# Branch announcements inside the expert passes of a two-layer decoder: all further passes against the first two

## Chip, cores and metric

One core of a Trainium2 chip runs the whole program. The time is the device time of one execution in microseconds; for the kernel before it is the median of three runs. Five engines work side by side: PE (TensorE, matrix products; its weight loads are counted apart as PEld), DVE (VectorE), ACT (ScalarE), POOL (GpSimd, which does almost nothing here) and SP (SyncE, which issues nearly all DMAs). Every engine has its own instruction stream and its own sequencer.

## What is computed

Two decoder layers over 256 tokens of width 1024, fp32. Each layer is a token mixer with four kinds of attention, then cross-attention into 256 memory tokens, then a hierarchical mixture of experts. Only the last part matters here:

```python
g_idx = jnp.argmax(g_logits, axis=-1)                      # 1 of 8 groups per token
top_val, top_idx = lax.top_k(e_logits, TOP_K_IN_GROUP)     # 2 of the group's 4 experts
hid = jax.nn.silu(jnp.einsum('sd,edf->sef', xs, w_gate)) * jnp.einsum('sd,edf->sef', xs, w_up)
return jnp.einsum('sef,efd->sd', hid * gates[:, :, None], w_down)
```

There are 32 experts in 8 groups of 4; each has a gate, an up and a down matrix of 1024 x 256 (1 MB each). How many tokens fall to an expert is known only at run time.

## The kernel before

The two layers run one after the other; each is `attention` and then `moe`. In `moe` the eight groups are served in an order that a table fixes (`SERVED`); `expert(g)` serves one. A pass over a group takes up to 32 tokens for each of its four experts, side by side on the four 32-column quarters of the PE array:

- `up_to` (L1277) multiplies the gathered tokens by the gate and the up weights,
- `silu` on ACT (L1281) and `act` on DVE (L1284) make the hidden values, `turned` (L1290, L427) transposes them,
- `down` multiplies by the down weights (L1306), splits the result in two parts on ACT and DVE (L1310, L1311) and scatters it back to the tokens (L1322, L1327).

The first pass (tokens 0 to 31 of every expert) is always run. If an expert of the group has more than 32 tokens, further passes c = 1 to 7 follow, for tokens 32c to 32c+31. They are nested conditional blocks which `over` writes: the block of pass c is entered if the group's largest count exceeds 32c, and the block of pass c+1 stands inside the block of pass c. So every group carries the code of seven further passes, and a group with no more than 32 tokens for any expert jumps over all of it. PE, ACT, DVE, POOL and SP each take that branch for themselves (line L1368 in the profile, COMPARE_BRANCH).

The count is loaded into a register of each engine (L1397). `foresee` (L1359 to L1365) is the announcement: on PE alone it writes a marker ahead of a later branch, which names that branch and says by the register whether it will be taken. In PE's stream this is two instructions: a register operation (L1363 ALU_OP) and a prefetch hint (L1604 BRANCH_PREFETCH_HINT). The hint tells the sequencer to fetch the code at the branch's target early if the branch will be taken. The announcement needs a label, and the label is handed to the `tc.If` of the block.

The first branch of a group (pass 1) is announced while `up_to` runs, by `tell`. The branch to pass c+1 is announced from inside the block of pass c, by the function that `over` hands to `f`:

- in `whole`, the usual case, `down` calls it between its first and its second half of down products (argument `between`);
- one group of the second layer is in `SPREAD`: group 0, served third. Its passes 1 to 3 are divided. `part` does gate and up and calls the announcement at its very start; `rest` does the down part later, in a second chain of three nested blocks (`top=3`), and announces as `whole` does. Passes 4 to 7 of that group go through `whole`.

Weights come in 1 MB pieces by DMA that SP issues (L275) in the order of one long list, each as soon as a buffer is free. `free` gives the gate and up buffers of a group back after the chain of passes, and the down buffers at the group's end. A pair of comparisons on SP (L274) leaves out experts without tokens.

Of the kernel before, what the change touches and what calls it, by code (L numbers as in the profile page):

```python
# [170 lines left out]
def trunk(ctx, tc, a, out, dbg=None, depth=DEPTH):  # L171
# [922 lines left out]
    def moe(l, pz, pb):  # L1094
# [264 lines left out]
        def foresee(rv, n):  # L1359

            marks[0] += 1
            label = f"m{l}_{marks[0]}"
            tc.mark_branch_hint_location(label, rv > n, engines=[mybir.EngineType.PE])  # L1363
            return label

        def over(rv, f, c=1, label=None, top=7):

            with tc.If(rv > 32 * c, label=label):  # L1368
                nxt = []
                f(c, lambda: nxt.append(foresee(rv, 32 * c + 32)) if c < top else None)  # L1370
                if c < top:
                    over(rv, f, c + 1, *nxt, top=top)

# [30 lines left out]
        def expert(g):  # L1404
# [4 lines left out]
            with tc.manual_schedule(engines={mybir.EngineType.Activation}):  # L1409
# [52 lines left out]
                with apart():  # L1462
                    over(full[g], part if wide else whole, label=label[0])
            free(g, 0, 8)
            pinned[1].close()
            if wide:
                with apart():
                    over(full[g], rest, top=3)
# [28 lines left out]
        for t in range(2):  # L1497
            o, src = ff[:, t], sums(t)
            mv, r = stats(src)
            for h in range(2):  # L1500
                c = slice(h * 512, (h + 1) * 512)
# [106 lines left out]
```

## Time and profile before

| what | value |
|---|---|
| median of three runs | 1011.58 us |
| the three runs | 1015.21, 1004.90, 1011.58 us |
| profiled execution, its own time | 1013.67 us |
| its span, first to last instruction | 1011.9 us |
| lying around the span | 1.8 us |
| PE busy | 923.1 us, 91% of the span |
| bytes moved by DMA | 272.59 MB, 269 GB/s over the span |
| instruction fetches of PE (queue q8) | 86, 1.41 MB |
| PE branches at L1368 that were executed | 30 |
| PE announcements that were executed | 24 |

The expert part of the first layer lies at about 275 to 510 us of the span, that of the second at about 765 to 995 us. A row of the profile names the line, the engine and the operation, what is written and read, and how often; "<-" in a wait names what ended it. A "q" behind an engine's name is its sequencer: PEq L1368 is PE's branch. Queue q1 carries the program's data, queue q8 the code that PE fetches, queue q14 the code of other engines. A hint's line in the profile is L1604, since it is placed when the program is closed.

### The profile page before, as it was taken

How to read it: one execution, taken by the hardware profiler on the slowest of the kernel's cores; microseconds unless marked ns; L12 is line 12 of the kernel's file. 1: busy time of each engine (PE TensorE's matmuls, PEld its weight loads, DVE VectorE, ACT ScalarE, POOL GpSimd, SP SyncE). 2: the span in 40 equal slices, each digit the busy share in tenths (PEclk: the TensorE clock that was granted, in tenths of full speed). 3: DMA queues.
4: the chain of work that ended last, by engine and by line, in shares of the span. 5: the costliest groups of instructions: out<-in, count | busy, mean ns of one | idle time of the engine just before them, and what ended most of it. 6: DMA issues, size and time to landing. Idle time of an engine off the chain costs nothing. (4 is left out here: it accounts for less than half of the span.)

```text
span 1011.9 us, 19936 instructions
## 1 busy us (share of the span) xinstructions
PE 923.1 (91%) x7948; PEld 688.2 (68%) x7948; DVE 503.3 (50%) x1258; ACT 340.9 (34%) x736; POOL 0.2 (0%) x4
## 2 busy tenths in 40 slices
PE   7899999999998688989899999999999888997885
PEld 7888987898754354856368899789885564444541
DVE  5755755544653333323466575554465414644434
ACT  5454855343411121011144475435442121121111
POOL 0000000000000000000000000000000000000000
PEclk9999999999999899999999999999999999999998
DMA  9842334538769988999786244553784994719995
GB/s 351 343 147 99 134 128 161 209 125 331 293 268 422 424 348 367 424 425 420 250 336 229 108 147 180 174 208 110 288 351 196 421 387 183 318 58 421 422 363 203
DMA packets 43774, 272.59 MB, mean 269 GB/s; under 512 B 4832, under 2 KB 5344, under 8 KB 13280
## 3 DMA queue, kind: packets, MB, share of 16 engines
q1 hardware_dynamic: 43472, 270.26, 68.2%
q8 instruction: 86, 1.41, 0.5%
q14 instruction: 72, 0.59, 0.2%
q10 hardware_dynamic: 144, 0.33, 0.1%
HBM read 269.52 MB, written 1.05 MB: 267 GB/s over the span
## 5 line engine op out<-in xcount | busy, mean ns | idle before, releaser
L432 DVE SCALAR_TENSOR_TENSOR wl<-main,wh 128x1024 fp32r<-128x1024 f32 (+1 forms) x93 | 112.2, 1211 | 112.1 <-ACT wh L431 111.9
L431 ACT ACTIVATE wh<-main 128x1024 fp32r<-128x1024 f32 (+1 forms) x93 | 97.3, 1052 | 116.5 <-PE bank L438 68.3
L437 PE MATMUL bank<-xh,wh 128*128 128x256 f32 x368 | 108.8, 298 | 5.6 <-ACT xh L488 3.6
L438 PE MATMUL bank<-xl,wh 128*128 128x256 f32 x368 | 105.8, 288 | 1.0 <-DVE xl L432 0.6
L439 PE MATMUL bank<-xh,wl 128*128 128x256 f32 x368 | 104.9, 286 | 0.0
L1277 PE MATMUL bank<-ext,xg 128*32 128x256 f32 x912 | 88.2, 392 | 2.9 <-DMA ext<-exp 2.8
L1327 DVE TENSOR_TENSOR ff<-ff,bank 128x512 f32<-128x512 f32 x84 | 53.2, 681 | 49.9 <-PE bank L1322 49.9
L437 PEld LDWEIGHTS bank<-xh,wh 128*128 128x128 f32 x368 | 71.1, 194 | 7.0 <-ACT xh L488 4.1
L438 PEld LDWEIGHTS bank<-xl,wh 128*128 128x128 f32 x368 | 71.3, 194 | 2.2 <-DVE xl L432 0.9
L439 PEld LDWEIGHTS bank<-xh,wl 128*128 128x128 f32 x368 | 71.4, 194 | 0.1
L1277 PE MATMUL bank<-main,xg 128*32 128x256 f32 x640 | 66.1, 384 | 2.4 <-DMA main<-exp 2.4
L460 ACT ACTIVATE xg<-bank,prmb 128x128 f32<-128x128 f32 x64 | 24.0, 456 | 123.3 <-PE bank L1227 117.2
L1310 ACT ACTIVATE y<-bank,sm 128x512 fp32r<-128x512 f32 (+1 forms) x46 | 30.7, 669 | 103.5 <-PE bank L1306 76.1
L1322 PE MATMUL bank<-y,dt 128*128 128x512 f32 (+1 forms) x184 | 56.9, 422 | 7.9 <-DVE y L1311 7.2
L1306 PE MATMUL bank<-ext,dn 128*32 128x512 f32 (+1 forms) x212 | 46.6, 670 | 17.5 <-PEq L1368 6.8
L437 PE MATMUL bank<-wh,oh 128*128 128x512 f32 (+1 forms) x160 | 60.9, 380 | 0.0
L439 PE MATMUL bank<-wh,ol 128*128 128x512 f32 (+1 forms) x160 | 59.1, 369 | 0.0
L1322 PEld LDWEIGHTS bank<-y,dt 128*128 128x128 f32 x184 | 29.6, 188 | 43.2 <-ACT y L1310 16.4
L438 PE MATMUL bank<-wl,oh 128*128 128x512 f32 (+1 forms) x160 | 59.0, 369 | 0.0
L1277 PEld LDWEIGHTS bank<-ext,xg 128*32 128x32 f32 x912 | 42.6, 112 | 22.5 <-issue 4.7
L1227 PEld LDWEIGHTS bank<-dn,xhat 128*128 128x128 f32 x448 | 51.1, 192 | 5.8 <-issue 4.9
L1227 PE MATMUL bank<-dn,xhat 128*128 128x128 f32 x448 | 53.7, 278 | 0.0
(300 smaller groups left out, 2008.7 us busy)
## 6 DMA issues: line engine op xcount, KB each, us to landing
ext<-exp SPq DMA_DIRECT2D x75, 1024.0 KB, 16.6
main<-exp SPq DMA_DIRECT2D x54, 1024.0 KB, 12.8
main<-wsq SPq DMA_DIRECT2D x33, 1024.0 KB, 5.0
main<-win SPq DMA_DIRECT2D x22, 1024.0 KB, 6.8
M<-exp SPq DMA_DIRECT2D x17, 1024.0 KB, 15.0
VM<-exp SPq DMA_DIRECT2D x8, 1024.0 KB, 17.1
xx<-exp SPq DMA_DIRECT2D x7, 1024.0 KB, 14.0
M<-wsq SPq DMA_DIRECT2D x5, 1024.0 KB, 7.1
```

Of the source, the lines that this page charges most:

```text
L431: ACT.activation(hi, src, AF.Copy, scale=scale)
L432: DVE.scalar_tensor_tensor(lo, src, scale, hi.bitcast(F32), op0=ALU.mult, op1=ALU.subtract)
L437: PE.matmul(psum, lh, rh, start=first, stop=False, skip_group_check=True)
L438: PE.matmul(psum, lh, rl, start=False, stop=False, skip_group_check=True)
L439: PE.matmul(psum, ll, rh, start=False, stop=last, skip_group_check=True)
L460: ACT.activation(dst, src, AF.Identity, bias=b, scale=g)
L1227: PE.matmul(b[:, k * 128:(k + 1) * 128], xhat[:, t, c:c + 128], d[:, t], start=(t == 0 and k == 0), stop=(t == 1), skip_group_check=True)
L1277: PE.matmul(pg[m * i:m * i + m, which * S:(which + 1) * S], x[:, k, m * i:m * i + m], w[:, k], start=(k == 0), stop=(k == 7), skip_group_c ...
L1306: PE.matmul(b[m * i:m * i + m], ht[:, f * 128 + m * i:f * 128 + m * i + m], w[:, o:o + n], start=(f == 0), stop=(f == 1), skip_group_check ...
L1310: ACT.activation(hi, b, AF.Copy, scale=gate)
L1322: PE.matmul(bs[t], dt[:, t * 128:(t + 1) * 128], y[i], start=(i == 0 and not held), stop=(i == 1), skip_group_check=bool(held))
L1327: DVE.tensor_add(o, o, bs[t])
```

## The change

`over` hands out the announcement only in the block of pass 1. The branch into pass 1 (announced by `tell`) and the branch into pass 2 (announced from the block of pass 1) stay as they were. The branches into passes 3 to 7 are no longer announced, and their blocks get no label.

```diff
             with tc.If(rv > 32 * c, label=label):
                 nxt = []
-                f(c, lambda: nxt.append(foresee(rv, 32 * c + 32)) if c < top else None)
+                f(c, lambda: nxt.append(foresee(rv, 32 * c + 32)) if c == 1 else None)
                 if c < top:
                     over(rv, f, c + 1, *nxt, top=top)
```

On PE 81 pairs of instructions leave the program, 162 in all: five for each of the sixteen groups (blocks of passes 2 to 6) and one in the second chain of the divided group. No other engine gains or loses an instruction. Everything that stands behind a removed pair moves up in PE's stream: ten instructions for each group, 152 by the last one.

The first place is the divided group of the second layer on PE: the end of pass 2's gate and up part, the branch into pass 3, that pass's start. (f is the choice of tokens that gathers them from xhat; xx holds the gathered tokens.) Before:

```order
L1277 MATMUL bank_3_64<-M_0_119,xx_0_69 32x256
L1277 MATMUL bank_3_64<-R_0_76,xx_0_69 32x256
L1368 COMPARE_AND_BRANCH
L1363 REGISTER_ALU
L1604 BRANCH_PREFETCH_HINT
L1227 MATMUL bank_5_66<-f_61_0_13925,xhat_0_77 128x128 x8
L1227 MATMUL bank_2_63<-f_61_0_13925,xhat_0_77 128x128 x8
```

And now:

```order
L1277 MATMUL bank_3_64<-M_0_119,xx_0_69 32x256
L1277 MATMUL bank_3_64<-R_0_76,xx_0_69 32x256
L1368 COMPARE_AND_BRANCH
L1227 MATMUL bank_5_66<-f_61_0_13805,xhat_0_77 128x128 x8
L1227 MATMUL bank_2_63<-f_61_0_13805,xhat_0_77 128x128 x8
```

The pair behind the branch is gone; it announced the next branch, the one into pass 4. The same pair is gone one block earlier, where it announced the branch into pass 3. Nothing else changes its place relative to its neighbours.

The second place is the divided group's later chain on PE, pass 2's down part, between its two halves (VM and ext hold down weights). Before:

```order
L1306 MATMUL bank_2_63<-ext_1_13934,f_61_1_13926 32x512
L1363 REGISTER_ALU
L1604 BRANCH_PREFETCH_HINT
L1306 MATMUL bank_7_68<-VM_0_75,f_61_1_13926 32x512
L1306 MATMUL bank_7_68<-KT_0_74,f_61_1_13926 32x512
```

And now:

```order
L1306 MATMUL bank_2_63<-ext_1_13814,f_61_1_13806 32x512
L1306 MATMUL bank_7_68<-VM_0_75,f_61_1_13806 32x512
L1306 MATMUL bank_7_68<-KT_0_74,f_61_1_13806 32x512
```

The pair between the halves is gone; it announced the chain's branch into pass 3.

## The prediction

> **What bounds the kernel now.** I read the page first, then the chain of work that ended last, then busy time and DMA by stretch for the second layer's experts, then PE's branches one by one.
>
> ```profile
> span 1011.9 us, 19936 instructions
> ...
> 910.52 0.75 PE bank L1322 x2
> ...
> 912.46 20.29 DMA main<-exp
> ...
> 985.96 6.99 DMA VM<-exp
> ...
> 992.99 1.90 PE bank L1306 x10
> ```
>
> The chain says that the end is set by weights that stream in from 912 to 993 us, and that the stream started when PE's work of 910.5 us had given buffers back. So the question for the second layer is what delays PE before 911 us.
>
> ```profile
> 840.00:846.00 6.00, 5.50 (x104) 3.09 (x100) 0.00 (x0) 1.75 (x5) 0.00 (x0) 1.00 0.01 4
> ...
> 890.00:900.00 10.00, 8.41 (x140) 4.43 (x142) 1.45 (x6) 2.27 (x6) 0.00 (x0) 1.00 0.01 2
> ...
> 912.00:930.00 18.00, 13.85 (x171) 8.67 (x163) 6.94 (x22) 2.16 (x6) 0.00 (x0) 0.94 1.01 421
> ```
>
> The last column is GB/s. DMA moves 421 GB/s from 912 on, but 4 GB/s at 840 to 846 and 2 at 890 to 900: all buffers are full, and DMA waits for PE. PE's own waits from 770 to 907 us are twelve rows, none for a DMA; the first and the last of them:
>
> ```profile
> PE bank L1306 <- ACTq L1368: 3.4, 2, 1.7
> ...
> PE bank L1322 <- ACT y L1310: 0.3, 1, 0.3
> ```
>
> In that stretch a microsecond that PE loses is a microsecond lost at the end; after 912 us DMA is the limit and short PE waits are covered.
>
> **The change, part by part.** First, what runs of it. Executed branches and announcements on PE, whole program, then the divided group's stretch from 807 to 868 us:
>
> ```profile
> L1368 PEldq COMPARE_BRANCH  x30: 68/365/5925, 282.9 to 989.4; - x30
> ...
> L1604 PEldq BRANCH_PREFETCH_HINT  x24: 32/38/44, 278.9 to 982.5; - x24
> ...
> L1368 PEldq COMPARE_BRANCH  x8: 68/78/367, 807.9 to 861.4; - x8
> ...
> L1604 PEldq BRANCH_PREFETCH_HINT  x5: 32/32/35, 808.2 to 856.3; - x5
> L1363 PEldq ALU_OP  x5: 37/37/37, 808.1 to 856.2; - x5
> ```
>
> Sixteen of the 24 are the groups' first announcements, which stay. Five lie in the divided group: three in its first chain (ahead of passes 2, 3 and 4) and two in its second. The remaining three belong to the three groups that run one further pass; each is announced from the block of pass 1 and stays. So the change takes away three executed announcements: two in the first chain (ahead of passes 3 and 4), one in the second (pass 3). Two of the three branches are not taken: the count is above 96, the code goes straight on, and such branches lasted 68 to 78 ns. They lose nothing. **One taken branch loses its announcement**: the one into pass 4, at 846.1 us, which jumps over the code of four passes.
>
> *The announcements themselves.* 3 x (0.037 + 0.032) = 0.2 us of PE's sequencer. In the first chain it runs ahead of products still queued; I count -0.1 us.
>
> *The branch at 846.1 us.* Its row, and what PE's code queue q8 did between the announcement and the branch:
>
> ```profile
> L1368 PEldq COMPARE_BRANCH  x1: 367/367/367, 846.1 to 846.1; - x1
> ...
> DMA packets 12, 0.04 MB, mean 3 GB/s; under 512 B 8, under 2 KB 8, under 8 KB 8
> ...
> q8 instruction: 1, 0.02, 0.5%
> ```
>
> One code fetch in 12.8 us, and the branch then took 0.37 us. No taken long jump without an announcement exists in this trace. The nearest rows are announced ones whose fetch came only after the branch had begun: one with DMA idle (377.5 us, 11 GB/s), two with DMA full (446.1 us at 425 GB/s, 921.4 us at 419).
>
> ```profile
> L1368 PEldq COMPARE_BRANCH  x1: 3631/3631/3631, 377.5 to 377.5; - x1
> ...
> DMA packets 5, 0.04 MB, mean 11 GB/s; under 512 B 1, under 2 KB 1, under 8 KB 1
> ...
> q8 instruction: 1, 0.02, 1.7%
> ...
> L1368 PEldq COMPARE_BRANCH  x1: 5811/5811/5811, 446.1 to 446.1; - x1
> ...
> DMA packets 343, 2.51 MB, mean 425 GB/s; under 512 B 38, under 2 KB 38, under 8 KB 38
> ...
> L1368 PEldq COMPARE_BRANCH  x1: 5925/5925/5925, 921.4 to 921.4; - x1
> ...
> DMA packets 344, 2.52 MB, mean 419 GB/s; under 512 B 38, under 2 KB 38, under 8 KB 38
> ```
>
> Bounds: 0.37 us if the target is there anyhow, 5.93 us at worst. I take 3.63 us, since DMA is idle around 846 us too (3 and 11 GB/s). Not all of it is lost. PE went on after the branch only when DVE had made the last hidden values:
>
> ```profile
> L1368 PEldq EVENT_SEMAPHORE  x1: 51/51/51, 847.6 to 847.6; - x1
> ...
> PE bank L1290 <- DVEq L1368: 0.9, 1, 0.9
> ```
>
> The branch would end at 846.07 + 3.63 = 849.7 us instead of 846.4; PE's next step stood at 847.6. So the loss is 849.7 - 847.6 = **2.1 us**; by the bounds 0 to 846.07 + 5.93 - 847.6 = 4.4 us. It lies in the stretch where PE sets the pace, and the buffers that the group gives back at 848 us come that much later, so I let it through whole.
>
> [...]
>
> *Everything behind moves up.* PE's code comes in pieces. In the second layer's attention part, a stretch with no branches:
>
> ```profile
> 526.50:753.40 226.90, 223.83 (x1509) 196.92 (x1508) 131.95 (x300) 113.47 (x255) 0.00 (x0) 0.99 0.56 203
> ...
> q8 instruction: 12, 0.20, 0.3%
> ```
>
> 1509 products and 1508 weight loads in 12 fetches are one fetch for 251 instructions. Each group stands 10 instructions earlier than the one before it, 152 at the end, so where an announcement and its branch fall in such a piece is dealt anew: whether the next sequential piece is fetched ahead of the announced one or not. PE's waits at these branches now, of the whole program, then the longest branch that ended in a wait for ACT, and two single waits for PE's own branch:
>
> ```profile
> PE bank L1306 <- PEq L1368: 12.1, 6, 4.0
> PE bank L1306 <- ACTq L1368: 11.7, 7, 1.7
> ...
> L1368 PEldq COMPARE_BRANCH  x1: 2416/2416/2416, 786.7 to 786.7; - x1
> ...
> PE bank L1306 <- ACTq L1368: 1.6, 1, 1.6
> ...
> PE bank L1306 <- PEq L1368: 3.5, 1, 3.5
> ...
> PE bank L1306 <- PEq L1368: 2.3, 1, 2.3
> ```
>
> Seven groups wait some 1.7 us (11.7 in 7), ended by ACT's own turn at the block's end, though PE's branch took up to 2.4 us; the dearest wait for PE's own branch, behind the 5.81 us one, is 4.0 us; those at 377.5 and 398.3 us are 3.5 and 2.3. So a re-dealt group costs between 1.7 and 4.0 us, up to 2.3 either way. I expect the 5.81 us branch to gain that (-2.3), one or two others to lose as much, and DMA to hide part of both in the first layer. I take 0, with -4.6 and +4.6 as the ends: two groups either way (2 x 2.3).
>
> *Sum.* -0.1 + 2.1 + 0 = +2.0 us. On the profiled execution, 1013.67 us (1011.9 of span and 1.8 around it), that is 1015.7. That execution lies 2.1 us above the median of the runs shown; on the median, 1011.58, the sum gives **1013.6 us**. The three runs before differ by 10.3 us, about 1%, which is what a measurement of this kernel can tell from no change.
>
> **Rivals.**
>
> [...]
>
> *The new layout gives back more than the branch takes.* The three dear waits for PE's own branch fall to the 1.7 us of the others: (4.0 - 1.7) + (3.5 - 1.7) + (2.3 - 1.7) = 4.7 us, time 1013.6 - 4.7 = 1008.9. For it: they are the three dearest, and a re-dealt fetch is likelier to come out nearer the common case. Against: all three lie in the first layer, where DMA is full for most of the time and PE waits for weights besides.
>
> *The layout turns against it: slower by over 1%.* When the sequential piece is asked for just ahead of the announced one, and DMA is full, the announced piece comes second and the branch takes 5.8 us or more. Price 2.3 us for each group that waits 1.7 now. It decides from four of the seven: 2.0 + 4 x 2.3 = 11.2 us, time 1022.8. For it: two branches show it already (446.1 and 921.4 us, 5.8 and 5.9 us). Against: the groups after 912 us are covered by DMA, which leaves five that could pay.
>
> **How the numbers follow.** The forecast, no change that can be told, centred at +2.0 us: 0.62. Target in the store: 0.13. Layout gives back: 0.15. Layout turns against: 0.10. The first two and four fifths of the third lie within 1% (0.62 + 0.13 + 0.12 = 0.87), less 0.02 on each side for the spread of the runs: 0.83. Faster by over 1%: 0.03 + 0.02 = 0.05. Slower by over 1%: 0.10 + 0.02 = 0.12. Range: down to 1013.6 - 4.6 (layout) less half of the runs' spread (5.1), 1004; up to 1013.6 + 2.3 (the dearer branch) + 4.6 (layout), 1020.5, the spread left out there since both are worst cases.
>
> **What would show it.** In the changed profile: 21 announcements at L1604 instead of 24, 30 branches still. The branch after pass 3 of the divided group, near 846 us, should last 3.6 us instead of 0.37, with one q8 packet inside it, and the wait of L1290 behind it should be a wait for PE's own sequencer. The stream of weights that starts at 912 should start some 2 us later and run the same 81 us. [...] If the times of other groups' first branches have moved by more than that in sum, the layout and not the lost announcement tells the result.

## The result, and the profile after

| | before | changed |
|---|---|---|
| median of ten runs each | 1011.56 us | 1021.18 us |
| lowest and highest | 1004.90 and 1015.40 us | 1015.79 and 1025.11 us |
| ratio to before, 95% interval | | 1.0103, 1.0078 to 1.0129 |
| profiled execution, its own time and span | 1013.67 and 1011.9 us | 1022.55 and 1020.8 us |

The change makes the kernel 9.6 us slower at the medians. The forecast was +2.0 us, and its range ended at 1020.5 us. Here and below, a ratio with its interval is worked out over all fast executions and is not the quotient of the two medians beside it; one execution of the first experiment, 1539 us long at a granted clock of 0.555, is left out.

First the rows on PE's sequencer that answer to those of before: the announcements, all branches, and then four single branches. The columns are the count and the shortest, median and longest duration in ns.

```profile
L1604 PEldq BRANCH_PREFETCH_HINT  x21: 28/39/44, 279.4 to 991.7; - x21
...
L1368 PEldq COMPARE_BRANCH  x30: 65/574/6570, 283.5 to 996.9; - x30
...
L1368 PEldq COMPARE_BRANCH  x1: 3711/3711/3711, 378.1 to 378.1; - x1
...
L1368 PEldq COMPARE_BRANCH  x1: 1730/1730/1730, 452.0 to 452.0; - x1
...
L1368 PEldq COMPARE_BRANCH  x1: 3350/3350/3350, 848.3 to 848.3; - x1
...
L1368 PEldq COMPARE_BRANCH  x1: 3408/3408/3408, 911.6 to 911.6; - x1
```

There are 21 announcements and 30 branches, as forecast. The branch that lost its announcement (848.3 us) took 3.35 us instead of 0.37. Several branches that were announced before and after differ all the same; two of them show both directions: the one at 446.1 us fell from 5.81 to 1.73 us, and the one at 904.7 us rose from 0.47 to 3.41 us.

Next, PE's waits of the changed kernel around the lost announcement, and its stretches there (in a stretch's row, the third number from the end is the granted clock, the last one GB/s):

```profile
PE bank L1290 <- DVE dt L1266: 2.6, 1, 2.6
...
845.00:852.20 7.20, 4.28 (x76) 2.11 (x68) 0.80 (x3) 0.38 (x1) 0.00 (x0) 1.00 0.02 6
852.20:859.00 6.80, 6.10 (x30) 1.67 (x34) 1.85 (x7) 1.07 (x2) 0.00 (x0) 0.50 0.94 346
859.00:866.00 7.00, 6.42 (x46) 2.49 (x42) 4.52 (x12) 1.63 (x3) 0.00 (x0) 1.00 1.00 420
```

PE was idle for 2.6 us where it had been idle for 0.9. For the 6.8 us that follow, the granted clock is 0.50. Before, the same work had the full clock; the row of before, and then the down products of that place in the changed kernel and in before:

```profile
848.40:855.20 6.80, 6.22 (x43) 2.52 (x43) 3.60 (x11) 1.76 (x3) 0.00 (x0) 1.00 0.96 367
```

```profile
L1306 PE MATMUL bank<-ext,f x16: 593/1061/1062, 853.6 to 859.3; 128*32 128x512 f32 x16
```

```profile
L1306 PE MATMUL bank<-ext,f x16: 592/592/617, 849.3 to 852.4; 128*32 128x512 f32 x16
```

30 products against 43 in 6.8 us, and one product in 1.06 us against 0.59. From the second chain's first branch to its second, PE took 9.43 us (852.14 to 861.57) where it had taken 6.62 (848.00 to 854.62): 2.8 us more, in a place where not one instruction was added.

The lag of the changed trace behind the trace of before, measured at the same branch in both, adds up so:

| branch, time before | lag | what grew it |
|---|---|---|
| 282.9 us, first of the first layer | 0.55 us | start of the run |
| 398.3 us, first layer's fifth group | 1.81 us | |
| 446.1 us, the sixth | 5.98 us | +4.2: behind the branch that is now 6.57 us and was 4.13 |
| 469.0 us, the seventh | 3.06 us | -2.9: the branch that is now 1.73 us and was 5.81 |
| 767.9 us, first of the second layer | 1.72 us | |
| 846.1 us, the lost announcement | 2.25 us | |
| 848.0 us, the next | 4.14 us | +1.9: the branch |
| 854.6 us, the one after | 6.95 us | +2.8: products at half clock |
| 904.7 us, fourth served group | 6.95 us | |
| 921.4 us, fifth served group | 9.12 us | +2.2: the branch that is now 3.41 us |

The weight stream that waits for PE moved with it. Before, it was already at 352 GB/s from 907 us on, earlier than the 912 us that the prediction read off the chain; in the changed trace it is idle until 912 and full from 918:

```profile
907.00:910.00 3.00, 3.00 (x29) 0.93 (x18) 2.59 (x14) 0.91 (x2) 0.00 (x0) 1.00 0.99 352
```

```profile
907.00:912.00 5.00, 4.95 (x36) 1.92 (x28) 1.92 (x3) 1.38 (x2) 0.00 (x0) 1.00 0.00 0
912.00:918.00 6.00, 2.76 (x26) 0.97 (x28) 4.36 (x16) 0.36 (x1) 0.00 (x0) 1.00 0.32 89
918.00:920.00 2.00, 2.00 (x16) 0.83 (x8) 1.56 (x5) 0.91 (x2) 0.00 (x0) 1.00 1.06 442
```

So the two traces tell of 1.9 + 2.8 + 2.2 us in the second layer. What they can't tell by themselves is whether the first layer's rows are typical, since each is one execution.

### The profile page after: what moved, and what is told of

Same layout as the page of the kernel before. It is cut to its first block, busy times and chain, and to the rows that moved or that the text cites. A ratio compares the mean times of both kernels' runs of the same rounds, so it can differ in the third digit from the quotient of the medians.

```text
span 1020.8 us, 19930 instructions
## 1 busy us (share of the span) xinstructions
PE 924.9 (91%) x7948; PEld 686.3 (67%) x7948; DVE 503.7 (49%) x1258; ACT 341.0 (33%) x736; POOL 0.2 (0%) x4
## 3 DMA queue, kind: packets, MB, share of 16 engines
HBM read 269.52 MB, written 1.05 MB: 265 GB/s over the span
## 5 line engine op out<-in xcount | busy, mean ns | idle before, releaser
L1306 PE MATMUL bank<-ext,dn 128*32 128x512 f32 (+1 forms) x212 | 46.3, 640 | 14.8 <-PEq L1368 8.1
L1311 DVE SCALAR_TENSOR_TENSOR y<-bank,sm,y 128x512 fp32r<-128x512 f32 (+1 forms) x46 | 33.3, 725 | 47.7 <-ACT y L1310 44.5
```

The source lines that it names most:

```text
L1306: PE.matmul(b[m * i:m * i + m], ht[:, f * 128 + m * i:f * 128 + m * i + m], w[:, o:o + n], start=(f == 0), stop=(f == 1), skip_group_check ...
L1311: DVE.scalar_tensor_tensor(lo, b, gate, hi.bitcast(F32), op0=ALU.mult, op1=ALU.subtract)
```

## The experiments

Each kernel has its own runs of the kernel before on the same chip; ratios are to those. "Stands elsewhere" means the place of an announcement in PE's instruction stream. I moved it by code that never runs, such as blocks of pass 7, so that what PE executes stays the same. Where a kernel has lines added, the rows' line numbers are higher by as many (L1308 and L1307 are L1306, L1291 is L1290).

### One part alone, and the change with one part undone

The first kernel is that of before with all 24 announcements in their place, but those ahead of passes 3 to 7 always say that the code goes straight on:

```diff
-                f(c, lambda: nxt.append(foresee(rv, 32 * c + 32)) if c < top else None)
+                f(c, lambda: nxt.append(foresee(rv, 32 * c + 32 if c == 1 else 0)) if c < top else None)
```

> The kernel before, with every instruction in its place; the announcements inside the blocks of passes 2 to 6 now always say that the branch will not be taken. So the code's layout is that of before and only the taken branch of the divided group (near 846 us) loses its early fetch. Theory A (the lost announcement counts, and PE's products run slowly for a while after the idle time): that branch takes 3.4 to 3.7 us, the products behind it (L1306) take 1.06 us each for some 5 us, and the kernel is 4 to 5 us slower than before, about 1016. Theory B (the layout makes the loss, the branch costs its wait alone, 2 us as predicted): 1013.5. Theory C (all of the loss is layout, the announcement did nothing): 1011.5, branch 0.4 us.

Measured: 1012.94 us against 1010.23, ratio 1.0037 (1.0018 to 1.0055), 2.7 us at the medians. The branch took 3.36 us at 837.5 us, PE idled 2.6 us behind it, and of the 6.8 us that followed half ran at half clock (mean 0.75):

```profile
L1368 PEldq COMPARE_BRANCH  x1: 3357/3357/3357, 837.5 to 837.5; - x1
...
PE bank L1290 <- DVE dt L1266: 2.6, 1, 2.6
...
841.50:848.30 6.80, 6.22 (x36) 1.97 (x37) 1.73 (x7) 1.42 (x3) 0.00 (x0) 0.75 0.94 358
```

So the lost announcement by itself costs about a third of the change's 1.03%. The rest must have another cause, and the new places of the code are the nearest.

The second is the changed kernel with that announcement kept (in the divided group's first chain, ahead of pass 4):

```diff
+        def tell_of(c, top):
+            return c == 1 and top == 7 or c == 3 and wide_now[0]
-                f(c, lambda: nxt.append(foresee(rv, 32 * c + 32)) if c == 1 else None)
+                f(c, lambda: nxt.append(foresee(rv, 32 * c + 32)) if tell_of(c, top) else None)
```

> The changed kernel with one announcement back, the one into pass 4 of the divided group; one announcement of that group's second chain, whose branch is not taken, is left out, so that all code behind stands where the changed kernel has it. Theory A: the branch near 848 us takes 0.4 us again, PE's products behind it stay at 0.6 us, and 4 to 5 us of the changed kernel's loss come back: about 1016.5. Theory B: only 2 us come back: about 1019. Theory C: nothing, 1021. All: the branch of the next group (near 905 to 912 us) still takes 3.4 us, since its announcement and its branch stand where the changed kernel has them.

Measured: 1015.22 us against 1010.23, ratio 1.0076 (1.0048 to 1.0104). The branch took 1.59 us and not 0.4: its code packet came 11.7 us after the announcement, where it came after 7.8 us before. PE idled 0.9 us, with no half clock behind it. The branch at 903.9 us still took 3.43 us. What is left, 0.76%, does not come from this announcement: from its branch to the second chain's second one 8.6 us passed, as in before. What came back, 0.27%, is less clear: with six executions the interval overlaps that of the changed kernel.

The third gives the divided group of the changed kernel four announcements back that decide nothing (eight instructions, two of them executed), so that the branch at 911.6 us stands eight places later:

```diff
+            return c == 1 or top == 3 and c == 2 or 3 < c < top and wide_now[0]
```

> The changed kernel with eight instructions more in the divided group: three pairs in blocks that never run, one pair in the second chain (its branch is not taken). Passes 3 and 4 stay unannounced. Everything from the group served fourth on stands eight instructions later. That group's taken branch, 3.4 us in the changed kernel against 0.47 before, stands at the edge of a code piece there by my count. If the place in the piece makes that branch slow, it takes 0.5 us here and the kernel gains 2.5 to 3 us on the changed one, about 1018.5; if the loss follows from something earlier (a later DMA, the branch at 848), it stays at 3.4 us and 1021.

Measured: 1018.6 us against 1010.23, ratio 1.0102 (1.0072 to 1.0131). The branch fell to 0.47 us, so its place alone had lost its announcement. Whether that place is the edge of a code piece is not shown: the expectation has it from a count of mine, and no trace tells where a piece ends. In the changed kernel no code packet came between announcement and branch; here one did:

```profile
DMA packets 0, 0.00 MB, mean 0 GB/s; under 512 B 0, under 2 KB 0, under 8 KB 0
```

```profile
L1372 PEldq COMPARE_BRANCH  x1: 466/466/466, 908.1 to 908.1; - x1
...
q8 instruction: 1, 0.02, 1.1%
```

The time did not fall, though. The branch at 968.1 us now took 5.9 us (0.71 in the changed kernel). The eight places need not be the reason: in the changed kernel with two announcements moved, below, where it stands 512 places later and not eight (near two code packets, by the estimate given there), it took 6.0 us. The price of the one branch isn't told by this run.

### Which branch the layout costs

The branch into pass 2 of the first layer's fourth group (377.5 us before) took 3.6 us in before's profile and 3.7 in the changed one, so the two traces show no difference there. In the profile of the first experiment, whose layout is that of before, it took 0.43. The two profiles from the announcement to the branch, before and then that one:

```profile
q1 hardware_dynamic: 152, 1.02, 47.6%
q14 instruction: 1, 0.01, 0.7%
```

```profile
q1 hardware_dynamic: 146, 0.99, 46.1%
q8 instruction: 1, 0.02, 1.2%
q14 instruction: 1, 0.01, 0.6%
```

With the one the announced code came in time (the q8 row), with the other no packet came before the branch. Two kernels move this announcement and bring the code behind back to its place. (The first also moves the two groups ahead up, by 10 and 20 places, as the change does; their branches took 1.08 and 2.55 us, against 1.04 to 1.56 and 2.01 to 2.45 in the seven profiles of before's layout. The second also moves the next group, by 10.) The edit to before that both share, with the first one's numbers (`SPARE`: unread transposes in a group's pass 7; `BARE`: groups whose announcements ahead of passes 3 to 7 are left out; none of either runs there):

```diff
+BARE = [(0, 0), (0, 1), (0, 2)]
+SPARE = {(0, 3): 15}
...
+                f(c, lambda: nxt.append(foresee(rv, 32 * c + 32)) if c < top and (c == 1 or not bare[0]) else None)
...
+                elif top == 7 and spare[0]:
+                    b = banks.get()
+                    for _ in range(spare[0]):
+                        PE.transpose(b[:, 0:128], ident, ident)
+                    banks.put(b)
```

> The kernel before, with every announcement that it executes. Only code that never runs is shorter in the first three groups of the first layer (30 instructions) and as much longer in the fourth, so that the fourth group's announcement into its second further pass stands 30 instructions earlier, where the changed kernel has it; all groups behind stand where they stand before. Theory (the place of the announcement costs, not its absence): that branch, 0.43 us in two profiles of this layout and 3.63 in one, takes 3.6 to 3.8 us and PE idles 3.5 us there; the time is 1.5 to 4 us above before, since some runs of before lose it too. Rival (the rest of the change's cost lies behind this group): the branch may take what it likes, the time is that of before within 1 us.

Measured: 1012.75 us against 1009.30, ratio 1.0038 (1.0019 to 1.0058), 3.5 us. The row of the branch and PE's wait behind it:

```profile
L1370 PEldq COMPARE_BRANCH  x1: 3411/3411/3411, 374.7 to 374.7; - x1
...
PE bank L1308 <- PEq L1370: 3.3, 1, 3.3
```

Nothing that PE executes differs from before; 30 instructions of place cost as much as the lost announcement of the first experiment. The other way:

```diff
+BARE = [(0, 3), (0, 4)]
+SPARE = {(0, 2): 10}
```

> The other way: the same announcement 20 instructions later than before (the next group's 10 later), by code that never runs; all behind stands where it stands before. Theory: the branch takes 0.43 us in this layout in every run, PE's idle time there falls under 0.5 us, and the time is 0.5 to 3 us below before. Rival: the time is that of before within 0.5 us.

Measured: 1009.20 us, ratio 1.0000 (0.9979 to 1.0020); the branch took 0.43 us. The expected gain of 0.5 to 3 us isn't there. The reason stands in the other profiles of before's layout: of seven, the fetch was missed in one, which was the profile that I predicted from. Measured in the trace, from the start of the last code packet to this announcement, in all fourteen profiles of the study:

| from the last code packet to the announcement | profiles | branch |
|---|---|---|
| 0.82 to 0.98 us (four kernels with the changed kernel's place) | 4 | 3.41 to 3.81 us |
| 1.46 us (before) | 1 | 3.63 us |
| 1.60 to 1.92 us | 9 | 0.43 to 0.56 us |

An announcement that came less than 1.5 us after the start of the last code packet was lost at this branch. The changed kernel's place lies ahead of that edge, before's place lies close to it. Why it is lost isn't shown: the packets took 0.94 to 0.96 us, so in before's profile the last one had been over for 0.5 us. Nor is the edge the same elsewhere. At the branch of 846.1 us an announcement 1.46 us behind a code packet was kept (0.37 us, in the first run with eight steps of DVE, below); at that of 921.4 us announcements 1.05 to 2.58 us behind one were lost in the changed kernel and the three made from it (3.2 to 3.8 us).

The changed kernel with both of its misplaced announcements moved (the first layer's fourth group's and the second layer's fourth served group's), all else left alone or moved by 256 or 512 places (near one and two code packets, by an estimate from the 251 products and weight loads for one fetch in the trace of before):

```diff
+SPARE = {(0, 2): 25, (0, 3): 103, (1, 2): 4, (1, 3): 124}
```

> The changed kernel, without the three announcements, with code that never runs added at four places, so that two announcements stand elsewhere: the first layer's fourth group's 50 instructions later, the second layer's fourth served group's 8 later; all other groups stand in their pieces as in the changed kernel. Theory: the two branches fall from 3.7 and 3.4 us to under 0.5, only the lost announcement is left, and the time is 3 to 5 us above before (ratio 1.003 to 1.005, as where that announcement alone was made idle) and not 9.6. Rival (other branches, or the new order of fetches at large, cost): the time stays at that of the changed kernel, 1.009 to 1.011.

Measured: 1014.75 us against 1009.30, ratio 1.0049 (1.0030 to 1.0067): half of the change's cost is gone, without one announcement given back. The two branches took 0.43 and 0.46 us. The one that has no announcement took 3.90, PE idled 3.2 us, and 3.4 us at half clock followed (granted clock 0.50 from 848.5 to 851.9 us). What is left agrees with the first experiment (1.0037), within both intervals.

```profile
L1369 PEldq COMPARE_BRANCH  x1: 432/432/432, 377.4 to 377.4; - x1
...
L1369 PEldq COMPARE_BRANCH  x1: 459/459/459, 905.7 to 905.7; - x1
...
L1369 PEldq COMPARE_BRANCH  x1: 3901/3901/3901, 843.2 to 843.2; - x1
```

And a version that uses this: all announcements that are executed, and the dear ones moved. (The edit moves the groups behind the first layer's sixth by 272 places, 16 more than the 256 of the kernel above, so they don't stand as the expectation says.)

```diff
+BARE = [(0, 3)]
+SPARE = {(0, 2): 10, (0, 4): 96, (0, 5): 35, (1, 3): 99, (1, 4): 29}
```

> The kernel before with all its announcements, and code that never runs added at five places, so that the dear branches' announcements stand elsewhere: the first layer's fourth group's 20 instructions later, its sixth group's 186 later in its piece (just ahead of the piece's end, as in the three groups with the cheapest branches), the second layer's fifth served group's 198 later; all others stand in their pieces as before. Theory: the three branches fall to 0.43, 1.7 and under 3.5 us (0.43 or 3.6, 5.8 and 5.9 before), and the time is 3 to 6 us below before. Rival (weights set the pace in the first layer and behind 912 us of the second, so that PE's waits there are covered): within 1 us of before.

Measured: 1007.81 us, ratio 0.9983 (0.9967 to 1.0000). The three branches took 0.56, 1.46 and 1.01 us, about as expected or shorter, but the gain is 1.5 us at the medians and not 3 to 6, at the edge of what the runs can tell. So most of PE's waits there seem to be covered by the weight stream, as the rival had it. At the first layer's sixth group the traces show it: from that branch to the next group's it took 24.2 us here and 23.7 in the first experiment, where the branch took 5.84 us and not 1.46.

### What a short stall costs PE

The half clock behind the stall was seen in the trace; these kernels test that it is the idle time that brings it, and its price. They are the kernel before, with steps of DVE ahead of the second chain's first transposes, and no change to the branches:

```diff
                 def rest(c, hint):
+                    if c == 1:
+                        for _ in range(8):
+                            DVE.tensor_scalar(hw[c], hw[c], 1.0, None, op0=ALU.mult)
```

> The kernel before with eight extra DVE steps (times 1.0) on the hidden values of pass 1 of the divided group, just ahead of the second chain: PE has to wait some 2 us longer at L1290 near 848 us, with no branch and no code fetch involved. PE's code is unchanged. Theory A: the wait of 0.9 us becomes 2.5 to 3.3 us, the products behind it run at 1.06 us instead of 0.6 for some microseconds, and the kernel loses 4 to 5 us. Theory B: it loses what the wait grows by, 2 us, and the products stay at 0.6 us.

Measured: 1017.28 us, ratio 1.0079 (1.0055 to 1.0102). PE's idle time grew by 3.7 us (0.87 to 4.54), but the stretch to the next branch by 6.5 (13.1 for 6.62). Then once more, with two kernels beside it on the same chip: two steps instead of eight, and eight steps with twelve unread transposes on PE meanwhile.

> The eight steps alone once more, on the same chip as the two others: 5 to 8 us over before (1.005 to 1.008), 3.7 us of it delay, the rest products at half rate.

> The kernel before, with two idle steps of DVE instead of eight at the same place. Theory: PE's idle time of 0.87 us grows to some 1.8 us, its products behind stay at full rate, and the time rises by the 0.9 us of the two steps (ratio 1.000 to 1.002). Rival (any stall there costs near twice its length): 1.8 us.

> The kernel before, with eight idle steps of DVE (a product by 1.0) ahead of the divided group's last hidden values, as in the run that lengthened PE's idle time there to 4.5 us and took 6.5 us more for the stretch up to the next of its passes; now PE does twelve transposes that nobody reads in that time. The code behind is brought back to its place by code that never runs. Theory (PE's products run at half rate after the idle time): the same delay of 3.7 us, PE idle at most 1.5 us at a time, no product at half rate behind it, and 3.5 to 4.5 us in all over before, 2 to 3 us less than the eight steps without the transposes. Rival (the delay itself costs all of it): as with the eight steps alone.

Measured: eight steps 1016.85 us against 1009.86, ratio 1.0073 (1.0058 to 1.0088); two steps 1.0003 (0.9985 to 1.0021); with twelve transposes 1.0067 (1.0045 to 1.0088). The wait ahead of the transposes and the stretch behind it, for eight steps, two steps, and twelve transposes:

```profile
PE bank L1290 <- DVE prmb L1462: 4.5, 1, 4.5
...
844.70:851.50 6.80, 6.02 (x30) 1.68 (x34) 0.86 (x2) 1.07 (x2) 0.00 (x0) 0.50 1.02 428
```

```profile
PE bank L1290 <- DVE prmb L1462: 1.9, 1, 1.9
...
845.90:852.70 6.80, 6.14 (x42) 2.54 (x43) 3.16 (x10) 1.76 (x3) 0.00 (x0) 1.00 0.98 410
```

```profile
PE bank L1291 <- DVE prmb L1470: 2.2, 1, 2.2
...
847.00:850.40 3.40, 3.25 (x16) 0.79 (x20) 0.00 (x0) 0.10 (x1) 0.00 (x0) 0.50 1.00 424
```

1.9 us of idle time left the clock alone. The twelve transposes ran one behind another in 1.5 us, less than I had counted on, and left 2.2 us: 3.4 us at half clock instead of 6.8, and a time that can't be told from that of eight steps. By the time alone the rival stood; the clock's row says that the test was too weak. So the same with 28 transposes:

```diff
+                        b = banks.get()
+                        for _ in range(28):
+                            PE.transpose(b[:, 0:128], ident, ident)
+                        banks.put(b)
```

> As the run with eight idle steps of DVE and twelve transposes, but with 28 transposes on PE: twelve took 1.5 us and left PE idle for 2.2 us, behind which its products ran at half rate for 3.4 us all the same. By 0.125 us each 28 last 3.5 us and leave under 0.5 us. Theory (half rate after idle time): no product of the divided group at half rate, and the stretch from the first branch of its second chain to the next takes 10.3 us (6.62 before, and 3.7 of delay) instead of 11.9 with twelve and 13.2 with none; the time is 3.5 to 4.5 us above before (ratio 1.003 to 1.005). Rival (the delay alone costs it): the ratio stays at 1.007.

```profile
PE bank L1291 <- DVE prmb L1470: 0.4, 1, 0.4
...
848.70:855.50 6.80, 6.17 (x42) 2.55 (x43) 2.07 (x4) 1.76 (x3) 0.00 (x0) 1.00 1.01 426
...
L1307 PE MATMUL bank<-ext,f x16: 592/592/617, 849.7 to 852.7; 128*32 128x512 f32 x16
```

Measured: 1013.52 us against 1009.73, ratio 1.0041 (1.0017 to 1.0065). The stretch took 10.30 us, as expected: 6.62 and 3.7 of delay. The rival's ratio of 1.007 lies just outside the interval. The same eight steps of DVE cost 0.73 to 0.79% with PE idle and 0.41% with PE busy. The difference is 3 to 4 us; the products at half clock make 2.9 us of it in the traces (a stretch of 13.2 us against 10.3).

## Why the prediction was wrong, step by step

**What bounds the kernel** was right. A microsecond that PE lost between 768 and 912 us came out at the end: in the last experiments 3.7 us of delay cost 3.8 us at the medians (28 transposes), and a stretch 6.6 us longer cost 7.0 (eight steps). The two traces alone would not show it: the lag of PE's branches is 9.1 us at 921 us, falls to 5.2 at 946, and is 8.9 us at the end of the span.

**What runs of the change** was right: three executed announcements fewer, two of them idle (their branches last 65 ns each), one that matters.

**The branch at 846.1 us** was right in its own duration (3.63 us forecast, 3.35 measured) and in the shift that follows (2.1 forecast, 1.9 measured). Its path was longer than forecast: L1290 was to wait for PE's own sequencer, but it waited for DVE's step L1266, which had itself waited for PE's branch:

```profile
851.82 0.29 DVE L1266 TENSOR_SCALAR dt<-cst 128x256 fp32r<-128x256 f32 x1 [1.48 <-PEq L1368]
```

The rival in which the branch stays near 0.4 us without its announcement (in the chances "target in the store", 0.13) fell: it took 3.35 us here and 3.36 in the first experiment. No run shows a store of PE's code or what it holds; what the traces show is code packets, one between announcement and branch before (841.1 us; branch 0.37 us) and one inside the branch in the changed trace (849.4 us).

**The first step that failed** is "Not all of it is lost ... So the loss is 849.7 - 847.6 = 2.1 us": the stall was priced at its own length. PE's idle time of 2.6 us was followed by 6.8 us at half clock, 2.8 us more. In the profiles of the first experiment and of the changed kernel with two announcements moved it is 3.4 us instead of 6.8. Alone, the announcement cost 0.37%, 2.7 us at the medians. The trace of before had this price in it, behind the very row that gave the 3.63 us: after a wait of 3.5 us the products took 1.06 us each, and 0.59 only some 4 us later.

```profile
381.71 0.92 PE L1306 MATMUL bank<-main,dn 128*32 128x512 f32 x1 [3.48 <-PEq L1368]
382.43 1.06 PE L1306 MATMUL bank<-main,dn 128*32 128x512 f32 x1
385.55 0.59 PE L1306 MATMUL bank<-main,dn 128*32 128x512 f32 x1
```

**The second step that failed** is "I take 0, with -4.6 and +4.6 as the ends: two groups either way". The dear branch at 446.1 us did gain (5.81 to 1.73 us), as expected, and others lost. But I took the 3.63 us of the branch at 377.5 us for a price that before always pays, and even listed it among the waits that a new layout could give back. It was an accident of the one profiled execution: six of seven profiles of that layout show 0.43. The change moves this announcement 30 instructions up, to where it was lost in all four profiles with that place, and that move cost 0.38%.

If the two prices add, 0.37% and 0.38% make 0.75 of the 1.03%; with both misplaced announcements moved the changed kernel comes to 1.0049, near the 1.0037 that is left for the lost announcement. The price in time of the second layer's fourth served group's branch was not separated; in the traces its stretch to the next group took 18.9 us in the changed kernel and 20.6 in the second experiment, against 16.7 to 17.1 in the twelve profiles where that branch was short. The branches at 398.3 and 446.1 us nearly cancel: with the changed kernel's layout the stretch behind the first took 51.6 to 51.9 us in four profiles of four, against 47.6 to 48.6 in the other ten, and the stretch behind the second 20.0 to 20.1 us against 22.9 to 24.2. The branch at 966.5 us (2.95 to 0.71) was not separated either.

The rival "the layout turns against it" was nearest, 1022.8 us with a chance of 0.10, but its mechanism was another. It had four groups paying 2.3 us each because the announced piece came second, its reading of the branches at 446.1 and 921.4 us, each with one code packet between announcement and branch and a second inside the branch (443.7 and 449.5, 919.0 and 925.0 us); here two announcements were lost altogether, and only the branch at 398.3 us looks like that rival (2.4 us longer).

How long PE can idle before its products slow down is open. The half clock came in stretches of 3.4 us (before, 381.8 to 385.2 us: granted clock 0.51) and 6.8 us (changed, 852.2 to 859.0 us: 0.50). Idle times of 2.2 and 2.6 us were enough for it, in the kernel with twelve transposes and in the changed one, while 3.2 us ahead of 915.6 us in the changed trace brought none (its row from 912 to 918 us has clock 1.00). The same place in the second experiment's profile, idle for 3.3 us, did bring one (clock 0.51 from 908.0 to 911.5 us). What decides between them isn't shown.

## What to carry to other kernels

Price a stall of PE with what follows it: here idle times from 2.2 us on were followed by a half clock in most cases (eight of the ten in the traces of before and of the changed kernel), and two of its stretches of 6.8 us cost 2.8 and 2.9 us. Add that, or give PE something to do meanwhile. Where code is fetched by branch, an edit that removes or adds instructions moves every announcement behind it, even where the edited code never runs. A row that comes once in one profile is no price: before a forecast rests on it, look for the same row in other executions, or give it a chance of its own.

## What was unexpected of the hardware

An announcement can be lost without a sign but the missing code packet (in the changed trace none from 906.5 to 911.6 us, and a branch of 3.41 us). Given 0.8 to 1.5 us after the start of another code packet, it was lost in five of five profiles at one branch; 1.6 to 1.9 us after, kept in nine of nine. Other branches had other limits, and the reason stays open. At the second layer's fourth served group it was lost in the two profiles where the branch stood as in the changed kernel (3.41 and 3.43 us), and kept in the two where it stood eight places further on (0.47 and 0.46 us).

PE's half clock came in stretches of 3.4 or 6.8 us behind idle times and followed some as short as 1.8 us (changed, 985.4 to 988.8 us: granted clock 0.50). With 28 unread fp32 transposes in place of the idle time it stayed away: the clock was 1.00 behind them, and 0.50 behind eight steps without them.
